# Making GpSimd work wait for the VectorE operation planned ahead of it (12 links in a one-core encoder layer)

## The chip, the cores and the metric

The kernel runs on one core of one Trainium2 chip. The metric is the device time of one execution in microseconds, from the first to the last work of the program; a trace of one profiled execution shows every instruction with its start and duration. Five engines work side by side, each through its own queue in order: TensorE (PE: matrix products and transposes), ScalarE (ACT), VectorE (DVE), GpSimd (POOL) and SyncE (SP, which issues nearly all DMA transfers here).

## The reference

One layer of a hybrid encoder, 512 tokens, width 1024, float32. An RMS norm and one wide input projection feed two branches; their gated sum goes through an output projection, and two normed residual additions close the layer.

```python
h = rms_norm(x, norm_pre[i])
(aq, ak, av, az, dq, dk, dv, db, da, dz, gate_att, gate_dn) = split_cols(h @ w_in[i])
...
o_att = gqa_attention(q, k, v)           # 8 heads, 2 kv heads, 128 wide
y_att = (o_att * jax.nn.silu(az)) @ w_br_att[i]
...
o_dn = bidir_gated_deltanet(qd, kd, vd, g, beta)   # 8 heads, chunks of 64, both directions
y_dn = (rms_norm(o_dn) * jax.nn.silu(dz)) @ w_br_dn[i]
mix = (jax.nn.sigmoid(gate_att) * y_att + jax.nn.sigmoid(gate_dn) * y_dn) @ w_out[i]
x = x + rms_norm(mix, norm_post[i])
x = x + rms_norm(jax.nn.sigmoid(x @ w_ple_gate[i]) * (p[i] @ w_ple_proj[i]), ple_norm[i])
```

In the delta rule each chunk needs a decay matrix exp(g_i - g_j) under a triangular mask, and the inverse of a unit triangular matrix.

## The kernel before

**Products in split form.** Every large product is made of three TensorE passes in fp32r: each operand is split into hi (rounded) and lo (the remainder). Activations lie transposed in SBUF as hi and lo; weights come as slabs of 128x1024 by DMA into `wraw`, two buffers. For each slab `split` (line 212) casts hi on ACT (`whi`) and subtracts lo = raw - hi (`wlo`), either on POOL (planned at 2.37 us) or on DVE (planned at 1.16 us), whichever is planned to end first, with a bias. `gemm_t` then issues 8 x 3 products of 512 columns per slab (lines 478 to 480). There are two `whi` and two `wlo` buffers, so that TensorE frees what the next split writes.

**The order of the work.** `Flow` is a planner written in Python. Generators for all parts of the layer (jobs of the weight stream in a fixed list, and side jobs for convolution tails, decay masks, the triangular inverse, attention heads and so on) call `op(engine, duration, ready time, function)`. The planner reserves the first free slot of that engine in planned time (`slot`, `fit`) and keeps the function in a heap; `flush` calls the functions in order of planned start (line 101, to which most trace rows are put down). So every engine's queue is in order of planned time; the real times differ. The framework adds semaphore waits only where data needs them.

**DVE and POOL.** `V` reserves DVE, `G` reserves POOL. `W` (line 171) reserves both for a DVE operation both of whose tensor inputs lie in SBUF: in planned time no POOL work stands beside it. The queues keep only the order on each engine, so in real time the two can still meet, or either can run ahead.

**The parts that the steps below touch.** `prep` (line 819) makes the decay masks, four tiles of 128x512 per head group g and direction d: a DMA brings a row broadcast (`u<-CI`), POOL masks it with `affine_select`, then either eight small exponentials on ACT (line 842) or one add on DVE (`exps2`, line 846, through `W`) and one exponential on ACT. `phase_a` (line 878) inverts the triangular blocks on DVE: 30 steps of a product and a subtraction (`step`, lines 928 and 930, through `W`), followed by transposes and TensorE block products (lines 972 to 1020). While this chain is planned, `split` prefers DVE. `conv_tail` runs four taps on DVE, a Tanh and one more DVE operation before TensorE transposes the result (line 713). `kv_tail` (line 1287) scales the rotated keys by their norms with a 128x256 product on DVE (through `W`), and TensorE transposes them (line 1309).

Of the kernel before, what the change touches and what calls it, by code (L numbers as in the profile page):

```python
# [11 lines left out]
AF = mybir.ActivationFunctionType  # L12
ALU = mybir.AluOpType
AX = mybir.AxisListType

S = 512
NT = 4
# [9 lines left out]
class Event:  # L27
    def __init__(self):
        self.t = None
# [5 lines left out]
class Flow:  # L35
# [7 lines left out]
    def __init__(self, slots):  # L43
        self.now = 0.0
        self.eng = {}
        self.slots = {k: [0.0] * n for k, n in slots.items()}
        self.parts = []
        self.later = []
        self.n = 0

    def spawn(self, gen, prio):
        ev = Event()
        self.n += 1
        self.parts.append([prio, self.n, gen, ("at", 0.0), ev])
        return ev
# [18 lines left out]

    def op(self, eng, dur, dep, fn, *a, **k):

        engs = eng if isinstance(eng, tuple) else (eng,)
        t, at = self.slot(engs, dur, dep)
        for e, i in zip(engs, at):
            self.eng[e].insert(i, (t, t + dur))  # L80
        if fn is not None:
            self.n += 1
            heapq.heappush(self.later, (t, self.n, fn, a, k))
        return t + dur

    def free(self, tag, t=None):
        self.slots[tag].append(self.now if t is None else t)
# [59 lines left out]
PR = dict(dec=5, dm1=7, y=9, conv=1, gate=0, kv=4, q=5, head=8, ple=5, prep=7, tab=9)  # L147
GAP = 0.0
EXPS = 0.0
X_DVE = ()  # L150
WARM = 8.2
W1 = 0
# [4 lines left out]
def layer(ctx, tc, x, p, wt, wba, wn, wpp, npre, rows, qkn, hd16, npost, pnorm, dnorm, cs, out):  # L157
    nc = tc.nc
    pe, act, dve, pool, sync = nc.tensor, nc.scalar, nc.vector, nc.gpsimd, nc.sync

    caps = {"wraw": 2, "whi": 2, "wlo": 2, "f2": 5, "c2": 4, "blk": 3, "gi": 2, "go": 2, "mm": 5, "aux": 3}
    F = Flow({**caps, **{f"u{i}": 1 for i in range(17)}})
    op, free, spawn = F.op, F.free, F.spawn

    def A(dur, dep, fn, *a, **k):
        return op("ACT", dur, dep, fn, *a, **k)

    def V(dur, dep, fn, *a, **k):
        return op("DVE", dur, dep, fn, *a, **k)

    def W(dur, dep, fn, *a, **k):

        return op(("DVE", "POOL"), dur, dep, fn, *a, **k)

    def G(dur, dep, fn, *a, **k):
        return op("POOL", dur, dep, fn, *a, **k)

    def Q(kb, dep, o, i, by=sync):

        t = op("DGE" if by is sync else "ACT", 0.46, dep, by.dma_start, o, i)  # L180
        return op("DMA", kb * 0.3, t + 0.5, None) + 1.3
# [6 lines left out]
    def tile(tag, shape, dt=F32):  # L188
        cnt[0] += 1
        return sb.tile(list(shape), dt, tag=tag, bufs=caps.get(tag, 1), name=f"{tag}_{cnt[0]}")  # L190

    def const(shape, name, dt=F32):
        return sb.tile(shape, dt, tag=name, bufs=1, name=name)

    def unit(i, shape, dt=F32):
        return tile(f"u{i}", shape, dt)
# [8 lines left out]
    def either(dep, *ways):  # L205

        w = min((F.fit(w[0], w[1], max(F.now + 0.2, dep + 0.15))[0] + w[1], i, w) for i, w in enumerate(ways))[2]
        return op(w[0], w[1], dep, *w[2:])
# [17 lines left out]
    def bc(a):  # L226
        return a.unsqueeze(2).to_broadcast([128, 4, 128])
# [333 lines left out]
    cj = const([128, 2, 4, 8, 2], "cj")  # L561
# [155 lines left out]
    def sumsq(pt, dst, dep=0.0):  # L717
        yield "get", "f2"
        sq = tile("f2", [128, 4, 128])
        ta = A(0.5, dep, act.activation, sq, pt, AF.Square)  # L720
        t = V(0.62, ta, dve.reduce_sum, dst, sq, axis=AX.X)
        free("f2", t)
# [88 lines left out]
    def r32(i):  # L811
        return slice(32 * i, 32 * i + 32)
# [6 lines left out]
    def prep(g, d):  # L819


        away = (g, d) == (1, 1)
        yield "ev", dec_ev
        if g == 1:
            yield "ev", E_ev[0, 1]
            yield "ev", sub_ev if d else spilled
        u = 16 if away else LTu[g, d]
        yield "get", f"u{u}"
        lt = unit(u, [128, 16, 128])
        sgn = 1 if d == 0 else -1  # L830
        for c in range(NT):
            E = lt[:, 4 * c:4 * c + 4, :]
            t = Q(2, late["CI"], E, CI[d, c, 4 * g:4 * g + 4].unsqueeze(0).to_broadcast([128, 4, 128]))
            yield "at", t - 1.0
            t = G(0.66, t, pool.affine_select, out=E, in_=E, compare_op=ALU.is_ge, fill=-1e30, base=0,
                  pattern=[[0, 4], [sgn, 128]], channel_multiplier=-sgn)

            def exps(E=E, c=c):
                for h in range(4):
                    for i in range(2):  # L840
                        e = E[:, h, i * 64:i * 64 + 64]
                        act.activation(e, e, AF.Exp, bias=cj[:, d, c, 4 * g + h, i:i + 1])

            def exps2(E=E, c=c):
                Eh = E.rearrange("p h (s i) -> p h s i", s=2)
                dve.tensor_add(Eh, Eh, cj[:, d, c, 4 * g:4 * g + 4, :].unsqueeze(3).to_broadcast([128, 4, 2, 64]))

            ta = F.fit("ACT", 1.94, max(F.now + 0.2, t + 0.15))[0] + 1.94
            tv = F.slot(("DVE", "POOL"), 0.68, t)[0] + 0.68
            if ta <= F.fit("ACT", 0.57, tv + 0.15)[0] + 0.57 + EXPS:  # L850
                t = A(1.94, t, exps)
            else:
                t = A(0.57, W(0.68, t, exps2), act.activation, E, E, AF.Exp)
            if away:
                t = Q(2, t, E1[c], E)
            tE[g, d, c] = t
        if away:
            free("u16", t)
            spilled.set(F.now)
            yield "get", f"u{LTu[g, d]}"  # L860
            lt = unit(LTu[g, d], [128, 16, 128])
            for c in range(NT):
                tE[g, d, c] = Q(2, tE[g, d, c], lt[:, 4 * c:4 * c + 4, :], E1[c])
        LTs[g, d] = lt
        yield "ev", nj_ev[g]
        for c in range(NT):
            E = lt[:, 4 * c:4 * c + 4, :]

            def scaled(E=E, c=c):
                for h in range(4):  # L870
                    act.activation(E[:, h, :], E[:, h, :], AF.Copy, scale=Nj[:, g, d, c, h:h + 1])

            tE[g, d, c] = either(tE[g, d, c], ("POOL", 1.05, pool.tensor_mul, E, E, bc(Nj[:, g, d, c])), ("ACT", 1.25, scaled))
        E_ev[g, d].set(F.now)
# [3 lines left out]
    def phase_a(g):  # L878
# [11 lines left out]
        for c in range(NT):  # L890
# [11 lines left out]
            for d in range(2):  # L902
                E = LT[d][:, 4 * c:4 * c + 4, :]
                t = V(0.62, tE[g, d, c], dve.tensor_mul, AT[g][d][:, 4 * c:4 * c + 4, :], qk, E)
                t = V(0.62, t, dve.tensor_mul, E, kk, E)
# [10 lines left out]
        t = Q(4, t2, dB[64:128].rearrange("(s q) j i -> q j s i", q=4).rearrange("q j s i -> (q j) s i"), lb)  # L916
# [3 lines left out]
        b, w, tt = (tile("blk", [128, 32, 32]) for _ in range(3))  # L920
        t = Q(4, max(tl + [t]), b, dB)
        yield "at", t - 0.5
        t = W(0.65, t, dve.tensor_scalar, out=w, in0=b, scalar1=-1.0, scalar2=None, op0=ALU.mult)
        t = W(0.15, t, dve.memset, w.rearrange("p a b -> p (a b)")[:, 0:1024:33], 1.0)

        def step(m):
            sh = [128, m, 31 - m]
            dve.tensor_tensor(out=tt[:, 0:m, 0:31 - m], in0=b[:, 0:m, m:m + 1].to_broadcast(sh),
                              in1=w[:, m:m + 1, m + 1:].to_broadcast(sh), op=ALU.mult)
            dve.tensor_sub(w[:, 0:m, m + 1:], w[:, 0:m, m + 1:], tt[:, 0:m, 0:31 - m])  # L930

        chains[0] += 1
        if g == 0:
# [1 line left out]
        for m in range(30, 0, -1):  # L935
            t = W(0.32 + 2 * m * (31 - m) * 0.00104, t - 0.1, step, m)
            yield "at", t - 1.0
        chains[0] -= 1
        t = Q(4, t, dW, w)
# [38 lines left out]
        t = A(0.5, 0.0, act.copy, M, m1)  # L978
# [11 lines left out]
        for d, P, Q_ in combos:  # L990
            t = V(0.62, 0.0, dve.tensor_scalar, out=LT[d][r32(P), :, r32(Q_)], in0=v1[r32(P)], scalar1=-1.0,
                  scalar2=None, op0=ALU.mult)
# [6 lines left out]
        for i in range(2):  # L999
# [9 lines left out]
            t = A(0.5, 0.0, act.copy, M2[:, 8 * i:8 * i + 8, :], m2)  # L1009
# [4 lines left out]
        for i in range(2):  # L1014
            yield "get", "aux"
            v3 = bank("aux", [128, 8, 64])
            for s in range(8):
# [3 lines left out]
                if s % 4 == 3:  # L1021
                    yield "pe", 0.62
                    yield "at", F.now + GAP
            t = V(0.62, 0.0, dve.tensor_scalar, out=LT[0][r64[0], 8 * i:8 * i + 8, r64[1]], in0=v3[r64[0]], scalar1=-1.0,
                  scalar2=None, op0=ALU.mult)
# [261 lines left out]
    def kv_tail(t, o, tev):  # L1287
# [7 lines left out]
        tq = A(0.35, 0.0, act.activation, sq, ks, AF.Square)  # L1295
        ts = V(0.35, tq, dve.reduce_sum, sak[:, t, :], sq, axis=AX.X)
        free("f2", ts)
# [88 lines left out]
    def att_head(h):  # L1386
# [14 lines left out]
        for t in range(NT):  # L1401
# [8 lines left out]
            rs = saq[:, t, h:h + 1]  # L1410
            te = V(0.62, 0.0, dve.reduce_max, mx, sc, axis=AX.X)
            te = V(0.15, te, dve.tensor_scalar, out=bi, in0=mx, scalar1=rs, scalar2=-1.0, op0=ALU.mult, op1=ALU.mult)
# [370 lines left out]
    for j in jobs:  # L1783
        f, a = j[0], tuple(j[1:])
# [77 lines left out]
```

## Time and profile before

| | |
|---|---|
| timed runs | median 771.64 us of 3 (769.33 to 776.71) |
| the profiled execution | 770.75 us, its span 769.0 us |
| busy PE, DVE, ACT, POOL | 753.4, 470.6, 344.4, 306.6 us |
| granted TensorE clock | 0.995 of full speed |

How to read the rows: start and duration in us; then engine, line, operation, tiles written and read (buffer numbers left out), shape and count. A bracket gives the engine's idle time ahead of the instruction and what ended it. Most lines are 101, where the planner calls each function; so the tile names tell the rows apart. Recorded spans on POOL are rough, and ends of products are modelled.

### The profile page before, as it was taken

The page shows a single profiled execution, that of the slowest core. Times are in us where ns is not written, and L with a number is a line of the kernel's source. Part 1 is how long each engine was busy: PE and PEld are TensorE (multiplying, and loading weights), DVE is VectorE, ACT ScalarE, POOL GpSimd, SP SyncE. Part 2 cuts the span into 40 slices and gives each one's busy share as a digit, 9 for nine tenths or more (in the row PEclk, how much of TensorE's full clock was granted, in tenths as well). Part 3 has the DMA queues.
Part 4 walks back from the last instruction along what each step waited for, and adds up shares of the span by engine and source line. Part 5 has one row for each costly group of instructions (what it writes and reads, how often), then busy time and mean ns, then how long its engine had stood idle before and what let it go on. Part 6 is the DMA issues. An engine that isn't in the chain of part 4 may idle for free.

```text
span 769.0 us, 11946 instructions
## 1 busy us (share of the span) xinstructions
PE 753.4 (98%) x4566; PEld 632.5 (82%) x4566; DVE 470.6 (61%) x910; ACT 344.4 (45%) x636; POOL 306.6 (40%) x276
## 2 busy tenths in 40 slices
PE   9998999999999999999999999999999999999995
PEld 7877888888879888888779988787888888888885
DVE  4548779978574667889494643637666753413434
ACT  6566563644544235332443145335566632332422
POOL 5255395311433227200441145556555424661511
PEclk9999999999999999999999999999999999999999
DMA  7453225664521224635521133424443256552313
GB/s 280 141 181 110 82 76 161 213 202 167 151 96 42 74 91 125 198 117 164 151 72 42 42 110 125 131 101 154 149 141 120 97 152 217 200 165 115 96 65 113
DMA packets 53899, 100.51 MB, mean 131 GB/s; under 512 B 21009, under 2 KB 21969, under 8 KB 53842
## 3 DMA queue, kind: packets, MB, share of 16 engines
q1 hardware_dynamic: 53554, 99.49, 39.7%
q8 instruction: 36, 0.59, 0.3%
q10 hardware_dynamic: 288, 0.26, 0.1%
q14 instruction: 21, 0.17, 0.1%
HBM read 80.83 MB, written 18.91 MB: 130 GB/s over the span
## 4 chain that ended last, share of the span: by engine, by line
PE 90%; DVE 4%; issue 2%; ACT 1%; POOL 1%; DMA 1%; POOLq 0%; DVEq 0%; SPq 0%; ACTq 0%
PE mm L478 15%; PE mm L480 15%; PE mm L479 15%; PE mm L498 4%; PE mm L500 4%; PE mm L499 4%; PE mm L516 3%; PE mm L517 3%; PE mm L518 2%; PE aux L1074 2%; PE mm L1434 2%; PE aux L1106 2%; PE aux L1054 1%; DVE f L101 1%; PE aux L1092 1%
## 5 line engine op out<-in xcount | busy, mean ns | idle before, releaser
L101 POOL TENSOR_TENSOR wlo<-wraw,whi 128x1024 fp32r<-128x1024 f32 x67 | 160.4, 2394 | 300.5 <-ACT whi L101 296.5
L478 PE MATMUL mm<-u,wlo 128*128 128x512 f32 x568 | 229.9, 405 | 2.0 <-POOL wlo L101 2.0
L480 PE MATMUL mm<-u,whi 128*128 128x512 f32 x568 | 222.1, 391 | 0.0
L479 PE MATMUL mm<-u,whi 128*128 128x512 f32 x568 | 221.4, 390 | 0.0
L101 ACT CAST whi<-wraw 128x1024 fp32r<-128x1024 f32 x84 | 88.2, 1050 | 130.8 <-PE mm L480 89.3
L480 PEld LDWEIGHTS mm<-u,whi 128*128 128x128 f32 x568 | 106.6, 188 | 23.3
L478 PEld LDWEIGHTS mm<-u,wlo 128*128 128x128 f32 x568 | 106.9, 188 | 22.1 <-POOL wlo L101 2.8
L479 PEld LDWEIGHTS mm<-u,whi 128*128 128x128 f32 x568 | 107.0, 188 | 19.3
L101 DVE SCALAR_TENSOR_TENSOR f<-mm,cw,f 128x510 f32<-128x510 f32 (+1 forms) x96 | 71.9, 749 | 22.5 <-ACT f L101 19.9
L101 DVE TENSOR_TENSOR u<-aux,u 128x512 fp32r<-128x512 f32 (+2 forms) x68 | 44.5, 672 | 27.9 <-ACT u L101 20.4
L498 PE MATMUL mm<-u,u 128*128 128x512 f32 (+1 forms) x136 | 52.0, 383 | 0.0
L500 PE MATMUL mm<-u,u 128*128 128x512 f32 (+1 forms) x136 | 51.4, 378 | 0.0
L499 PE MATMUL mm<-u,u 128*128 128x512 f32 (+1 forms) x136 | 51.2, 377 | 0.0
L101 POOL TENSOR_TENSOR u<-wraw,u 128x1024 fp32r<-128x1024 f32 x16 | 38.3, 2398 | 13.4 <-ACT u L101 13.3
L516 PE MATMUL mm<-whi,u 128*128 128x512 f32 x96 | 38.2, 398 | 0.0
L518 PE MATMUL mm<-whi,u 128*128 128x512 f32 x96 | 37.5, 391 | 0.0
L517 PE MATMUL mm<-wlo,u 128*128 128x512 f32 x96 | 37.5, 390 | 0.0
L101 ACT COPY c<-aux 128x512 f32<-128x512 f32 x18 | 10.6, 587 | 58.7 <-DVE f L101 36.4
L101 ACT CAST u<-aux 128x512 fp32r<-128x512 f32 (+1 forms) x36 | 20.0, 564 | 35.1 <-PE aux L1607 14.0
L101 ACT ACTIVATE f<-mm 128x512 f32<-128x512 f32 (+1 forms) x38 | 20.9, 562 | 24.5 <-PE mm L713 9.8
L101 ACT ACTIVATE mm<-f 128x512 f32<-128x512 f32 x24 | 14.4, 601 | 38.0 <-DVE f L101 34.1
L500 PEld LDWEIGHTS mm<-u,u 128*128 128x128 f32 x136 | 25.6, 188 | 4.9
(254 smaller groups left out, 1298.3 us busy)
## 6 DMA issues: line engine op xcount, KB each, us to landing
wraw<-in_wt_dram SPq DMA_DIRECT2D x72, 512.0 KB, 3.4
wraw<-in_wn_dram SPq DMA_DIRECT2D x28, 512.0 KB, 3.9
u<-CI SPq DMA_DIRECT2D x16, 256.0 KB, 4.7
u<-in_x_dram SPq DMA_DIRECT2D x4, 512.0 KB, 7.4
eD<-c SPq DMA_DIRECT2D x8, 256.0 KB, 2.3
gate_dz<-go SPq DMA_DIRECT2D x8, 256.0 KB, 2.0
gate_gB<-go SPq DMA_DIRECT2D x8, 256.0 KB, 2.3
gate_gA<-go SPq DMA_DIRECT2D x8, 256.0 KB, 2.0
```

The lines of the kernel that those rows point to most:

```text
L101: fn(*a, **k)
L478: pe.matmul(o, lo[:, k, :], mh(k), start=(k == 0), stop=False)
L479: pe.matmul(o, hi[:, k, :], ml(k), start=False, stop=False)
L480: pe.matmul(o, hi[:, k, :], mh(k), start=False, stop=(k == 7))
L498: pe.matmul(o, b, hi, start=(i == 0), stop=False)
L499: pe.matmul(o, a, lo, start=False, stop=False)
L500: pe.matmul(o, a, hi, start=False, stop=(i == 7))
L516: pe.matmul(o[t], b, hi, start=(k == 0), stop=False)
L517: pe.matmul(o[t], a, lo, start=False, stop=False)
L518: pe.matmul(o[t], a, hi, start=False, stop=(k == 7))
L1074: pe.matmul(pw[:, h, :], Vm[g][d][:, 4 * c + h, :], r[:, h, :], start=True, stop=True)
L1106: pe.matmul(oa[:, h, :], AT[g][d][:, 4 * c + h, :], w[:, h, :], start=True, stop=True)
```

## The change: a wait from POOL on the DVE operation planned close ahead

Where a POOL operation of at least 0.6 us (planned) is issued, and the last issued DVE operation that reserved both engines was planned to end less than 1.5 us ahead of its planned start, the POOL instruction gets an explicit semaphore dependency on that DVE instruction. The order on every engine and all planned times stay. `exps2` and `step` now return their last instruction, so that it can be waited for. The rule passes over POOL functions that return no instruction (the small norm helpers).

```diff
+SYNC = mybir.DependencyInfo(mybir.DependencyClass.Sync, mybir.DependencyReason.DATA)
...
+        self.shut, self.link = None, lambda a, b: None
...
         if fn is not None:
             self.n += 1
+            if eng == "POOL" and dur >= LONG:
+                fn = self.behind(t, fn)
+            elif engs[1:] == ("POOL",):
+                fn = self.shutting(t + dur, fn)
             heapq.heappush(self.later, (t, self.n, fn, a, k))
         return t + dur
+
+    def shutting(self, end, fn):
+        def f(*a, **k):
+            self.shut = end, fn(*a, **k)
+        return f
+
+    def behind(self, t, fn):
+        def f(*a, **k):
+            ins = fn(*a, **k)
+            if ins is not None and self.shut and self.shut[1] is not None and t - self.shut[0] < NEAR:
+                self.link(ins, self.shut[1])
+        return f
...
+LONG, NEAR = 0.6, 1.5
...
+    def link(later, ahead):
+        tc.add_manual_dep(later.ins, ahead.ins.name, SYNC, reason="not beside each other")
+
+    F.link = link
...
-                dve.tensor_add(Eh, Eh, cj[:, d, c, 4 * g:4 * g + 4, :].unsqueeze(3).to_broadcast([128, 4, 2, 64]))
+                return dve.tensor_add(Eh, Eh, cj[:, d, c, 4 * g:4 * g + 4, :].unsqueeze(3).to_broadcast([128, 4, 2, 64]))
...
-            dve.tensor_sub(w[:, 0:m, m + 1:], w[:, 0:m, m + 1:], tt[:, 0:m, 0:31 - m])
+            return dve.tensor_sub(w[:, 0:m, m + 1:], w[:, 0:m, m + 1:], tt[:, 0:m, 0:31 - m])
```

The change is described as touching 36 places. Walked through on the planner's list, the rule selects 12 in one program: eight `affine_select` of `prep` and four `wlo` subtractions.

## Rows read from the trace of the kernel before

**Rows 1.** The page, busy time of each engine: busy us, share, instructions
```profile
PE 753.4 (98%) x4566; PEld 632.5 (82%) x4566; DVE 470.6 (61%) x910; ACT 344.4 (45%) x636; POOL 306.6 (40%) x276
```

**Rows 2.** Timeline of TensorE, the stalls that DVE or POOL ended
```profile
56.99 0.50 PE L478 MATMUL mm<-u,wlo 128*128 128x512 f32 x1 [0.67 <-POOL wlo L101]
...
66.68 0.66 PE L713 MATMUL mm<-ident,u 128*128 128x128 f32 x4 [0.76 <-DVE u L101]
...
71.41 0.50 PE L478 MATMUL mm<-u,wlo 128*128 128x512 f32 x1 [1.31 <-POOL wlo L101]
...
400.44 0.44 PE L1309 MATMUL aux<-ident,f 128*128 128x128 f32 x2 [1.40 <-DVE u L101]
...
495.55 0.63 PE L1168 MATMUL mm<-ident,u 128*128 128x128 f32 x4 [0.82 <-DVE u L101]
```

**Rows 3.** Timeline of POOL, 51 to 62 us
```profile
51.62 0.63 POOL L101 TENSOR_SCALAR_AFFINE_SELECT u<-u 128x512 f32<-128x512 f32 x1
...
54.54 2.40 POOL L101 TENSOR_TENSOR wlo<-wraw,whi 128x1024 fp32r<-128x1024 f32 x1 [2.28 <-issue]
...
59.24 2.40 POOL L101 TENSOR_TENSOR wlo<-wraw,whi 128x1024 fp32r<-128x1024 f32 x1
```

**Rows 4.** Timeline of DVE, 51 to 66 us
```profile
51.64 1.16 DVE L846 TENSOR_TENSOR u<-u,cj 128x512 f32<-128x512 f32 x1 [0.42 <-POOL u L101]
...
59.46 2.74 DVE L846 TENSOR_TENSOR u<-u,cj 128x512 f32<-128x512 f32 x1
...
65.12 0.68 DVE L846 TENSOR_TENSOR u<-u,cj 128x512 f32<-128x512 f32 x1
```

**Rows 5.** Timeline of POOL, 394 to 405 us
```profile
397.39 2.38 POOL L101 TENSOR_TENSOR wlo<-wraw,whi 128x1024 fp32r<-128x1024 f32 x1
```

**Rows 6.** Timeline of DVE, 394 to 405 us
```profile
395.27 0.42 DVE L101 TENSOR_TENSOR f<-f,sak 128x256 f32<-128x256 f32 x1
...
397.99 2.06 DVE L101 TENSOR_TENSOR f<-f,sak 128x256 f32<-128x256 f32 x1
```

**Rows 7.** Timeline of POOL, 143 to 180 us
```profile
165.06 0.64 POOL L101 TENSOR_SCALAR_AFFINE_SELECT u<-u 128x512 f32<-128x512 f32 x1 [11.72 <-DVE blk L928]
...
175.37 1.58 POOL L101 TENSOR_SCALAR_AFFINE_SELECT u<-u 128x512 f32<-128x512 f32 x1 [1.53 <-DMA u<-CI]
```

**Rows 8.** Timeline of DVE, 143 to 180 us
```profile
166.79 0.39 DVE L930 TENSOR_TENSOR blk<-blk,blk 128x220 f32<-128x220 f32 x1
167.09 0.68 DVE L846 TENSOR_TENSOR u<-u,cj 128x512 f32<-128x512 f32 x1
...
173.87 0.69 DVE L846 TENSOR_TENSOR u<-u,cj 128x512 f32<-128x512 f32 x1 [2.25 <-POOL u L101]
...
175.24 1.22 DVE L101 TENSOR_TENSOR wlo<-wraw,whi 128x1024 fp32r<-128x1024 f32 x1
```

**Rows 9.** Timeline of ACT, 48 to 70 us
```profile
52.83 0.63 ACT L101 ACTIVATE u<-u 128x512 f32<-128x512 f32 x1 [0.40 <-DVE u L846]
53.37 1.03 ACT L101 CAST whi<-wraw 128x1024 fp32r<-128x1024 f32 x1
...
62.23 0.63 ACT L101 ACTIVATE u<-u 128x512 f32<-128x512 f32 x1 [1.47 <-DVE u L846]
...
65.30 0.60 ACT L101 ACTIVATE mm<-f 128x512 f32<-128x512 f32 x1 [0.52 <-DVE f L101]
...
67.80 1.03 ACT L101 CAST whi<-wraw 128x1024 fp32r<-128x1024 f32 x1
```

**Rows 10.** Timeline of TensorE, the first product with three of the slabs
```profile
63.04 0.39 PE L478 MATMUL mm<-u,wlo 128*128 128x512 f32 x1
...
177.55 0.39 PE L478 MATMUL mm<-u,wlo 128*128 128x512 f32 x1
...
407.42 0.48 PE L478 MATMUL mm<-u,wlo 128*128 128x512 f32 x1
```

**Rows 11.** One stretch: us, busy of PE, PEld, DVE, ACT, POOL, clock, DMA
```profile
143.00:193.00 50.00, 50.00 (x226) 41.36 (x225) 43.25 (x90) 24.99 (x52) 7.25 (x7) 1.00 0.61 199
```

## The prediction

> **What bounds the kernel now.** I read the page's busy times first: TensorE has work for 753.4 of 769.0 us [rows 1]. The other engines are at 40 to 61%, so an edit on VectorE (DVE) or GpSimd (POOL) pays only where TensorE stands still for them. The second view is TensorE's own timeline, searched for stalls that a DVE or POOL instruction ended. There are five [rows 2]: 0.67 us at 56.99 and 1.31 us at 71.41 for a POOL weight remainder (wlo), 0.76 at 66.68, 1.40 at 400.44 and 0.82 at 495.55 for a DVE operation. Their sum, 4.96 us, is about all that any change in the order of DVE and POOL can give; no other stall over 0.15 us was ended by either of them. The third view is the timelines of POOL, DVE and ScalarE (ACT) around the places touched.
>
> **Which places.** The planner is a fixed calculation, so the rule of the change can be walked through on the plan of before. It selects 12 POOL operations in one program (36 is three times that): eight `affine_select`, four weight subtractions. In the profiled run they fall into four kinds.
> (a) POOL started first and the DVE operation met it: 51.62 beside 51.64, 59.24 beside 59.46, 397.39 beside 397.99 [rows 3, 4, 5, 6].
> (b) DVE started first and POOL sat behind it anyway: three of the `affine_select` at 151 to 176, which took 1.3 to 1.6 us in place of 0.64 (1.58 at 175.37, behind the DVE subtraction of 175.24) [rows 7, 8].
> (c) The POOL operation was over before the planned DVE operation began, since DVE ran late: three places, 147.25, 149.05 and 165.06; the last stands in [rows 7], its DVE operation ran 166.79 to 167.18 [rows 8].
> (d) The DVE operation was long done: three places, 54.54 among them [rows 3].
>
> **Part 1, what (a) returns.** The masked decay add on DVE takes 0.68 us undisturbed, at 65.12, and took 1.16 at 51.64 and 2.74 at 59.46 [rows 4]: 0.48 and 2.06 lost to POOL. The 256-column product takes 0.42 at 395.27 and took 2.06 at 397.99 [rows 6]: 1.64 lost.
> *At 51.6:* the add ends 0.48 earlier. ACT waits for it at 52.83, casts whi at 53.37 right behind, and POOL's subtraction at 54.54 follows the cast's end (54.40) by 0.14 [rows 3, 9]. The delayed `affine_select` moves DVE's second add by 0.3, to an end near 53.7, still ahead of 54.1. So that wlo comes about 0.4 earlier, and of the stall of 0.67 about 0.4 goes.
> *At 59.2:* DVE's add ends near 60.14 in place of 62.20; the conv taps behind it start 2 us earlier. ACT, which sat 1.47 us at 62.23 for this add, goes on at 60.8; its Tanh at 65.30 comes to 63.4 [rows 9]. The transposes at 66.68 wait for the DVE operation behind that Tanh, so their 0.76 goes altogether. The next cast, at 67.80, comes up to 2 us earlier, and with it the wlo for which TensorE stalls at 71.41; TensorE itself arrives 0.4 + 0.76 earlier, so of the 1.31 about 0.85 goes. Price: POOL's own subtraction starts at about 60.2 and ends at 62.6 in place of 61.64; its slab is first used at 63.04 [rows 10], by 24 products counted from 56.99. The 0.4 left just covers it; if cover fails, TensorE stalls by what is missing, under 1 us. Behind it on POOL stands one `affine_select`, whose reader runs only at 66.55. POOL issues no DMA here; the weight load that SyncE starts when this subtraction ends moves by 1 us and is cast near 70, so it is hidden. Sum to 72 us: 0.4 + 0.76 + 0.85 = 2.0.
> *At 397.4:* the product ends near 398.4 and TensorE, done with its row of products at 399.04, doesn't stall at 400.44 [rows 2]: 1.4 gained. POOL's subtraction ends at 400.85 in place of 399.77; its slab is used at 407.42 [rows 10], so 6.6 us hide it. Behind it wait POOL's small scale operations, about 0.1 late.
>
> **Part 2, what the waits cost.** No row shows such a wait's own price. The nearest is the 0.14 from an ACT end to the POOL start it releases [rows 3, 9]; the lower bound is nothing, since in kinds (b) and (d) POOL starts no earlier today. Twelve times 0.14, 1.7 us, is the upper bound, were all on the path; none is, by the slacks above, so I take nothing. In (c) POOL now starts 2.1 us later each time, and DVE's next add, which needs that mask and is in order, waits with all behind it: at 167.09 [rows 8] it would come at about 167.7 (the chain step that met the mask at 165.20 gets 0.35 back first). Of the two others the same count gives -0.2 and +0.7. TensorE doesn't stall anywhere between 72 and 215 us; slabs made by DVE are ready 0.45 to 2.9 us ahead, 1.09 for the one subtracted at 175.24 and used at 177.55 [rows 8, 10]. Half a microsecond of DVE lateness is thus hidden there, and DVE's idle 2.25 at 173.87 [rows 8] absorbs some. In the stretch 143 to 193 DVE is busy for 43.25 of 50 us [rows 11], however, with a 30-step chain whose result TensorE takes in at 211 us, with no slack that I can see. A TensorE that arrives 2.0 earlier there can find DVE not 2.0 earlier. So the first gain lies between 0 and 2.0; I take 1.3, nearer the top because the ACT casts that DVE waits for move with TensorE.
>
> **A rule weighed.** The rows show the second to start waiting for the first: the add at 59.46 ended 0.55 after POOL's 61.64. [...]
>
> **Sum.** 1.3 + 1.4 = 2.7 us. The profiled execution took 770.75 us (span 769.0), so 768.0. The median of the three timed runs, 771.64, lies 0.9 above it, and the same subtraction from it gives 768.9; I stay with 768.0.
>
> **The rivals.**
> *More is gained.* All of the 2.0 is kept and the stall at 495.55 goes too: 770.75 - 4.2 = 766.5. For it: the casts follow TensorE. Against: nothing touched lies near 495. Chance 0.12.
> *No difference: the gain is given back.* TensorE runs ahead of its weights, the early gain dies at 211 and the later one at a slab that comes late after 400; nothing is kept of the 2.7, 770.75 - 0 = 770.8. For it: DVE's load in 143 to 193. Against: weights are cast when TensorE frees their buffer, so they follow it. Also here: the waits don't do what they say, because engine starts shift by some tenths between executions and (a) need not recur. Chance 0.24.
> *Slower: DVE waits for POOL that waits for DVE.* In the three places of (c) the new wait strings mask, add and chain together. Were the whole POOL delay, 2.17 + 2.04 + 2.12 = 6.3 us, passed on, less 1.09 of slack at 175.24, TensorE would lose 5.2, and with only the gain at 400 left: 770.75 + 5.2 - 1.4 = 774.6. It decides once DVE is over 1.09 us late at 175.24. For it: DVE is nearly full there. Against: the add waits only 0.6 to 0.9 by the count above, and 2.25 idle comes before 175.24. Chance 0.10.
> The forecast, a gain of 1.5 to 3.5 us, has the remaining 0.54.
>
> **How the numbers follow.** The forecast and the first two rivals hold 0.90 and their times lie between 766.5 and 770.8; runs of one kernel differ by more (769.33 to 776.71 before), so I set 764.5 to 773.5, which leaves out the slower case and far runs. Measurement can tell about 1%, 7.7 us, from no change. Faster than that needs more than all stalls in sight: 0.03. Slower than that needs the slower case at more than its price, every late POOL operation of (a) to (c), 16 us together, mostly unhidden: 0.03. Within 1%: 0.94.
>
> **What would show it.** Right: the adds at 51.6 and 59.5 and the product at 398 take 0.68, 0.68 and 0.42, each with its POOL operation behind; TensorE's stalls at 66.7 and 400 are gone and that at 71.4 is halved; the chain's DVE stretch shows idle of 0.6 to 0.9 before two adds, ended by POOL. Wrong: a new TensorE stall at 63 (subtraction late), at 150 to 180 (DVE late), or at 211 (the chain late), or any slab in that stretch that DVE delivers after TensorE asks.

## The result and the profile after

The median fell from 773.46 us (10 runs, 769.33 to 776.71) to 768.19 (10 runs, 765.57 to 771.05): a ratio of 0.9934, interval 0.9912 to 0.9957, so 3.3 to 6.8 us. A second measurement of the same kernel (below) gave 0.9967, interval 0.9949 to 0.9985. Both intervals hold the stretch from 0.9949 to 0.9957, 3.3 to 3.9 us; that is a rough common value and no interval of its own. The forecast was 2.7 us and 768.0. The change lies within the 1% that the prediction called no change, though both intervals leave out a ratio of 1.

The page after, the busy times [rows 1]. The profiled execution took 769.0 us:

```profile
span 767.3 us, 11952 instructions
...
PE 753.6 (98%) x4566; PEld 633.0 (82%) x4566; DVE 466.2 (61%) x910; ACT 344.1 (45%) x636; POOL 303.6 (40%) x276
```

DVE lost 4.4 us of busy time and POOL 3.0 without losing an instruction: the time in which one sat behind the other. TensorE's busy time is unchanged (753.4 and 753.6 us for the same 4566 products); what can have shrunk is its idle time.

The DVE operations that met POOL before [rows 4, 6, 8], timeline of DVE after:

```profile
51.09 0.69 DVE L873 TENSOR_TENSOR u<-u,cj 128x512 f32<-128x512 f32 x1 [0.95 <-POOL u L102]
...
58.45 0.68 DVE L873 TENSOR_TENSOR u<-u,cj 128x512 f32<-128x512 f32 x1
...
148.95 0.69 DVE L873 TENSOR_TENSOR u<-u,cj 128x512 f32<-128x512 f32 x1 [0.74 <-POOL u L102]
...
164.60 0.69 DVE L873 TENSOR_TENSOR u<-u,cj 128x512 f32<-128x512 f32 x1 [0.87 <-DMA wraw<-in_wt_dram]
...
397.39 0.43 DVE L97 TENSOR_TENSOR f<-f,sak 128x256 f32<-128x256 f32 x1
```

And their partners, timeline of POOL after [rows 3, 5, 7]:

```profile
51.85 0.63 POOL L102 TENSOR_SCALAR_AFFINE_SELECT u<-u 128x512 f32<-128x512 f32 x1 [0.79 <-DVE u L873]
...
59.27 2.41 POOL L102 TENSOR_TENSOR wlo<-wraw,whi 128x1024 fp32r<-128x1024 f32 x1 [1.05 <-issue]
...
163.93 0.63 POOL L102 TENSOR_SCALAR_AFFINE_SELECT u<-u 128x512 f32<-128x512 f32 x1 [12.45 <-DVE blk L957]
...
397.95 2.40 POOL L102 TENSOR_TENSOR wlo<-wraw,whi 128x1024 fp32r<-128x1024 f32 x1 [1.13 <-issue]
```

Read the two in pairs. The adds took 1.16 and 2.74 us before and the product 2.06; now 0.69, 0.68 and 0.43, and POOL starts 0.07, 0.14 and 0.13 us behind their ends (51.78, 59.13, 397.82). Note that for the subtractions at 59.27 and 397.95 the bracket says "issue", though the wait added here is what held them: that a start follows a DVE end by 0.14 is seen only by laying the two engines side by side.

TensorE's timeline after, its stalls [rows 2] and the products around 210 us:

```profile
55.92 0.50 PE L505 MATMUL mm<-u,wlo 128*128 128x512 f32 x1 [0.68 <-POOL wlo L102]
...
68.35 0.50 PE L505 MATMUL mm<-u,wlo 128*128 128x512 f32 x1 [0.28 <-POOL wlo L102]
...
207.67 1.29 PE L999 MATMUL aux<-blk,u 32*32 32x32 f32 x128
...
210.47 1.02 PE L1012 MATMUL aux<-u,c 32*32 32x32 f32 x96
...
213.10 0.45 PE L1012 MATMUL aux<-u,c 32*32 32x32 f32 x32 [1.62 <-issue]
...
398.05 0.39 PE L507 MATMUL mm<-u,whi 128*128 128x512 f32 x1
398.28 0.38 PE L1336 MATMUL aux<-ident,f 128*128 128x128 f32 x2
...
493.54 0.63 PE L1195 MATMUL mm<-ident,u 128*128 128x128 f32 x4 [1.01 <-DVE u L122]
```

Of the five stalls of before, the 0.76 at 66.68 and the 1.40 at 400.44 are gone, the 1.31 at 71.41 is 0.28, and those at 57 and 495 stay. A stall that [rows 2] did not list, because neither DVE nor POOL ended it, has grown to 1.62 us at 213.10. Following the n-th product of one trace to the n-th of the other gives the balance. TensorE is 1.02 us earlier at 14 us, ahead of any link; 3.06 earlier at 71; 2.17 earlier at 213; 0.60 at 218; 2.16 at 400; 1.96 at the end. So the early links gave 2.04 us, 2.46 were lost between 210 and 218, and the link at 398 gave 1.56.

### The profile page after: what moved, and what is told of

Read it like the earlier page. It is cut to its first block, busy times and chain, and to the rows that moved or that the text cites. A ratio compares the mean times of both kernels' runs of the same rounds, so it can differ in the third digit from the quotient of the medians.

```text
span 767.3 us, 11952 instructions
## 1 busy us (share of the span) xinstructions
PE 753.6 (98%) x4566; PEld 633.0 (82%) x4566; DVE 466.2 (61%) x910; ACT 344.1 (45%) x636; POOL 303.6 (40%) x276
## 4 chain that ended last, share of the span: by engine, by line
PE 89%; DVE 1%; ACT 1%; issue 1%; DMA 1%; POOL 0%; POOLq 0%; DVEq 0%; SPq 0%; ACTq 0%
PE mm L505 16%; PE mm L507 16%; PE mm L506 16%; PE mm L527 4%; PE mm L525 4%; PE mm L526 4%; PE mm L543 3%; PE mm L544 3%; PE mm L545 3%; PE aux L1101 2%; PE mm L1461 2%; PE aux L1133 2%; PE aux L1081 1%; PE aux L1119 1%; PE aux L1092 1%; PE mm L740 1%
```

## The experiments

All experiments but the last three leave the plan, the instructions and their order alone and only choose which of the 12 links are made: `link` is called for the m-th selected place if m is in a list. Places 1 to 3 lie at 51 to 59 us, 4 to 10 (the masks beside the triangular inverse) at 146 to 174, 11 and 12 at 366 and 397.

```diff
+                self.m += 1
+                if self.m in KEEP:
-                self.link(ins, self.shut[1])
+                    self.link(ins, self.shut[1])
```

**early**, the first three links alone.

```diff
+KEEP = (1, 2, 3)
```

> Only the three links before 62 us. Theory A (the gain is the TensorE stalls that GpSimd and VectorE cause near 57, 67, 71 and 400 us, and the mask links near 150 to 175 are free): the adds at 51.6 and 59.5 take 0.68 us, TensorE is 2.0 us earlier by 72 us than it was relative to its start of products, the stall at 400 stays at 1.4; total 1 to 2 us faster than before, ratio 0.997 to 0.999. Theory B (the mask links matter, because they keep GpSimd from the steps of the chain): under 1 us. Theory C (no part alone shows; before varies between executions): ratio 1.000.

Measured: 769.23 us against 772.35, ratio 0.9962, interval 0.9946 to 0.9979: 1.6 to 4.2 us, where 1 to 2 was expected. TensorE's timeline in this run:

```profile
56.06 0.50 PE L508 MATMUL mm<-u,wlo 128*128 128x512 f32 x1 [0.34 <-POOL wlo L102]
...
68.48 0.50 PE L508 MATMUL mm<-u,wlo 128*128 128x512 f32 x1 [0.24 <-POOL wlo L102]
...
212.61 0.45 PE L1015 MATMUL aux<-u,c 32*32 32x32 f32 x32 [0.97 <-issue]
...
398.30 0.44 PE L1339 MATMUL aux<-ident,f 128*128 128x128 f32 x2 [1.39 <-DVE u L124]
```

The stalls of 57 and 71 shrink and that of 66.7 is gone, while the one at 400 stays at 1.39: each link acts at its own place. At 212.61 only 0.97 us are lost, not 1.62.

**late**, the link at 397 alone.

```diff
+KEEP = (12,)
```

> Only the link near 397 us. Theory A: the key product at 398 takes 0.42 us and the stall of 1.4 us at 400 goes; nothing else changes, the stalls of 0.76 and 1.3 us near 67 and 71 stay; 1.4 us faster, ratio 0.998. Theory B: the same 1.4 us, since it says nothing of this place. Theory C: 1.000.

Measured: 769.36 against 772.35, ratio 0.9959, interval 0.9941 to 0.9977: 1.8 to 4.6 us where 1.4 was expected. TensorE's timeline:

```profile
65.98 0.66 PE L743 MATMUL mm<-ident,u 128*128 128x128 f32 x4 [0.74 <-DVE u L124]
...
70.70 0.50 PE L508 MATMUL mm<-u,wlo 128*128 128x512 f32 x1 [1.28 <-POOL wlo L102]
```

The early stalls are back as they were [rows 2], and nothing stalls at 400. Followed product by product, this trace gives back 1.6 us there, and loses about 1 us at the stall of 495, which the link doesn't touch. What the timed runs give beyond 1.6 has no place in this trace.

**masks**, places 4 to 10 alone, where the prediction saw only a price.

```diff
+KEEP = (4, 5, 6, 7, 8, 9, 10)
```

> Only the seven links on affine_select between 145 and 176 us. Theory A: the masks start 0.07 us behind their VectorE operation, the chain ends within 0.5 us of where it ended, TensorE doesn't stall in the stretch; 0 +/- 0.5 us, ratio 1.000. Theory B: the chain ends about 1 us earlier and 1 to 3 us come off the total, ratio 0.996 to 0.999. Rival slower: VectorE waits for masks and TensorE for slabs at 150 to 180; 1 to 5 us slower, ratio 1.001 to 1.007.

Measured: 770.88 against 772.35, ratio 0.9982, interval 0.9966 to 0.9998. The rival that strings DVE and POOL together is out: nothing is slower. In the trace the 30-step chain ends 0.3 us later than before, and all of TensorE's stalls stay, the one at 400 among them:

```profile
400.68 0.44 PE L1339 MATMUL aux<-ident,f 128*128 128x128 f32 x2 [1.41 <-DVE u L124]
```

So a gain of 0.2 to 2.6 us is measured, where Theory A expected 0 within 0.5 and Theory B 1 to 3. The size fits B, its mechanism doesn't, since the chain ends no earlier; no row shows how the gain could arise. That stays open.

**early_late**, all but places 4 to 10.

```diff
+KEEP = (1, 2, 3, 11, 12)
```

> All links but the seven on affine_select between 145 and 176 us. Theory A: as fast as the whole change, 2.7 to 5 us faster than before, ratio 0.993 to 0.997. Theory B: 1 to 3 us slower than the whole change.

Measured: 768.22 against 772.35, ratio 0.9932, interval 0.9911 to 0.9952. Without the seven mask links the gain is that of the whole change as first measured (0.9934), so what masks showed is not needed for it. Of the five, 2 and 11 are of kind (d) and no run took them alone. With six timed runs the interval is wide.

**none**, the control: the changed program with no link made, so the instructions and waits of before.

```diff
+KEEP = ()
```

> A control: the code of the change with no link kept, so that every engine's instructions and waits are those of before. Theory A: ratio 1.000 within its interval (the excess of about 1 us that each part alone showed over its stall is scatter). Rival (an offset between a new kernel and before in the way they are timed): 0.998 to 0.9985, and 1 to 1.4 us must be taken off every part's gain. The adds and the product take 1.16, 2.74 and 2.06 us again.

Measured: 771.68 against 771.58, ratio 0.9994, interval 0.9974 to 1.0014. No offset shows, but the interval also holds the 0.998 to 0.9985 of the rival, so it doesn't rule one out by itself. Set directly beside the control, which shares any such offset, the 12 times of after_again (below) lie 2.9 us lower on the mean (768.66 against 771.55), 1.7 to 4.1 by a 95% interval. That much comes from the waits and from nothing else in the change. TensorE's timeline:

```profile
63.66 0.66 PE L743 MATMUL mm<-ident,u 128*128 128x128 f32 x4 [0.71 <-DVE u L124]
...
68.38 0.50 PE L508 MATMUL mm<-u,wlo 128*128 128x512 f32 x1 [1.28 <-POOL wlo L102]
...
212.70 0.45 PE L1015 MATMUL aux<-u,c 32*32 32x32 f32 x32 [1.16 <-issue]
...
398.42 0.44 PE L1339 MATMUL aux<-ident,f 128*128 128x128 f32 x2 [1.41 <-DVE u L124]
```

It also answers a doubt of the prediction, whether engine starts shift between executions so that the meetings of kind (a) need not recur. They do recur: 1.17 and 2.74 us for the two adds and 2.05 for the product in this second execution of the old order, from DVE's timeline of this run:

```profile
56.43 2.74 DVE L876 TENSOR_TENSOR u<-u,cj 128x512 f32<-128x512 f32 x1
...
395.98 2.05 DVE L97 TENSOR_TENSOR f<-f,sak 128x256 f32<-128x256 f32 x1
```

**after_again**, the changed kernel itself once more, beside the control and on the same chip.

> The change once more, for its second trace. Theory A: ratio 0.992 to 0.996 again; no collision over 0.5 us on VectorE; the stall inside the second block product at about 213 us is again 0.7 to 1.6 us, ended about 1.4 us after the instruction fetch of 16 KB has landed; the drop of TensorE's clock behind it may or may not come back.

Measured: 768.13 against 771.58, ratio 0.9967, interval 0.9949 to 0.9985: 1.2 to 3.9 us. Its stall at 213 measured 1.90 us.

**early_again** and **late_again**, the same two parts once more.

> Only the three links before 62 us, once more. Theory A: 2.0 us at 72 us, less what the stall at 213 us takes back, 0.3 to 0.9 us and sometimes a drop of the clock: 0.5 to 2 us faster, ratio 0.9975 to 0.9995. Rival (more than the stalls is gained): 0.996 again.

> Only the link near 397 us, once more, since the first measurement gave 3.2 us (1.8 to 4.6) for a stall of 1.4 us. Theory A with scatter: 1 to 2.5 us faster, ratio 0.997 to 0.9985. Rival (the wait gives back more than the stall that a trace shows): 0.996 again.

Measured: early_again 769.37 against 771.62, ratio 0.9970 (0.9952 to 0.9988), late_again 770.11 against 771.62, ratio 0.9969 (0.9954 to 0.9985). Together with the first runs, early is worth between 1.6 and 3.7 us (both intervals hold 0.9952 to 0.9979) and late between 1.8 and 3.6 (0.9954 to 0.9977). The forecast had 1.3 and 1.4. In the repeat the stall at 213 was 0.78 with the early links.

**spread**: can the loss at 213 be had back? The 128 small products there are issued in four parts, with a planned gap behind each.

```diff
-GAP = 0.0
+GAP = 0.3
```

> The change, and the small block products of each inverse issued in quarters with one step of a large product between them. If the stall of 1.62 us at 213 us (and 0.35 at 383) is TensorE waiting for its own instructions, it shrinks to under 0.3 us, because the small products no longer use them up at 10 ns each: 1 to 3 us faster than the change, ratio to before 0.990 to 0.993. If it is a wait for data, it stays, and the inverse ends later: same or 1 us slower than the change.

Measured: 796.83 against 771.58, ratio 1.0327, interval 1.0297 to 1.0356. The stalls at 213 and 383 are gone, but the gaps move what the planner places later. Busy time by stretch (columns: us, busy of PE, PEld, DVE, ACT and POOL with their instructions, granted clock, DMA share, GB/s), spread first, then the changed kernel:

```profile
430.00:480.00 50.00, 38.00 (x261) 34.24 (x261) 24.43 (x75) 9.50 (x17) 2.53 (x2) 0.93 0.08 27
```

```profile
430.00:480.00 50.00, 50.00 (x273) 42.78 (x272) 23.23 (x56) 20.39 (x40) 20.93 (x17) 1.00 0.34 108
```

TensorE idles for 12 us of 50 where it never did before, among operations of the recurrence that other work used to fill; DMA carries 27 GB/s there in place of 108. A local cure that goes through the planner changes the whole order.

**v1_gap**: the same cure with one gap, in the middle of the second block product of each inverse only, on top of the change.

```diff
-                yield "at", F.now + GAP
+                yield "at", F.now + (0.3 if s == 7 else GAP)
```

> The change, and in the second block product of each inverse one step of a large product put in at half, ahead of the quarter in which TensorE stalled for 0.7 to 1.9 us. Theory (TensorE waits for its own instructions there): the stall at 213 us is under 0.8 us and no drop of the clock follows; up to 2 us faster than the change, ratio to before 0.990 to 0.995, unless the order behind it, which the planner lays anew from there, costs as much as it did with all quarters spread. Rival (a wait for data): the stall stays at 1.6.

Measured: 767.08 against 771.62, ratio 0.9940, interval 0.9915 to 0.9965; the profiled span is 764.0 us. It is the fastest median here, but its interval overlaps that of the change, so it is not shown to be faster. TensorE's timeline, and the stretch around it:

```profile
210.44 0.75 PE L1012 MATMUL aux<-u,c 32*32 32x32 f32 x64
...
212.02 0.90 PE L1012 MATMUL aux<-u,c 32*32 32x32 f32 x64
```

```profile
210.00:220.00 10.00, 10.00 (x167) 7.87 (x166) 8.39 (x12) 3.82 (x6) 4.62 (x2) 1.00 0.23 81
```

With large products issued between the halves TensorE doesn't stall, and the clock stays at 1.00 through the stretch.

**gate_first**: the stall at 495 is named for a DVE operation, but that one stood behind a gate load. The first gate load of each head group is asked for ahead of a planned wait.

```diff
+        ahead = yield from gate_in("dz", 4 * g)
...
-            zt, tz = yield from gate_in("dz", 4 * g + h)
+            zt, tz = ahead if h == 0 else (yield from gate_in("dz", 4 * g + h))
```

> The change, and the first gate tile of each half of the delta branch loaded before the wait for the scaled output in place of after it. The stall of 0.6 to 1.9 us at 494 us, whose VectorE operation waited up to 4.1 us for that load, goes: 0.6 to 1.5 us faster than the change, ratio to before 0.991 to 0.9935.

Measured: 770.20 against 771.58, ratio 0.9985, interval 0.9965 to 1.0006. A miss: with all links in place, it is slower on the mean than after_again, which was measured with it, by 1.7 us (0.5 to 3.0). DVE's timeline in this run:

```profile
494.06 0.76 DVE L122 SCALAR_TENSOR_TENSOR mm<-mm,dnn,gi 128x512 f32<-128x512 f32 x1 [4.51 <-DMA gi<-gate_dz]
```

DVE waits 4.51 us for the gate, and TensorE's stall behind it is 2.13. Before it waited 3.20, but in the control, without this step, 4.50: the wait varies by itself. Nor did the step bring the load forward in real time. SyncE issues it here, and in the control, by its timelines:

```profile
488.42 0.42 SPq L122 DMA_DIRECT2D gi<-gate_dz  x1
```

```profile
487.00 0.38 SPq L124 DMA_DIRECT2D gi<-gate_dz  x1
```

That is 1.1 us before DVE falls idle (489.55 and 488.10) in both. So the experiment didn't test an earlier load. What the traces show of the stall at 495 is that it ends with this load, and that DVE starts 4.3 us behind the issue before and 5.6 in the control and here. Why the load takes longer in one execution than in another is open. The planner also laid out anew what follows from 300 us on.

## Why the prediction was right, and where its steps were not

**What bounds the kernel, and the places.** Held. In the traces only stalls of TensorE, and its clock, moved the time; the 12 places were those found by walking through the plan, and the time came from places of kind (a) alone.

**Part 1, at 51.6.** Of the 0.67 about 0.4 was to go; in the trace after, 0.68 stays. The step that failed is "the add ends 0.48 earlier, ACT waits for it". The add did end earlier, but in this execution ACT stood behind its own exponentials, by its timeline after [rows 9]:

```profile
49.85 2.03 ACT L869 ACTIVATE u<-u,cj 128x64 f32<-128x64 f32 x8 [0.43 <-POOL u L102]
...
52.36 1.03 ACT L122 CAST whi<-wraw 128x1024 fp32r<-128x1024 f32 x1
```

They had waited 0.43 for a mask, and so the cast kept its place. In seven other traces with this link the stall is 0.34, 0.36, 0.43, 0.19, 0.77, 0.68 and 0.30; in five without it 0.67, 0.52, 0.86, 0.72 and 0.85. On the mean it falls from 0.72 to 0.47 over all thirteen; in one execution the gain is not certain.

**Part 1, at 59.2.** Held, by its own steps: the add takes 0.68, the Tanh and the transposes behind it come earlier, the 0.76 goes, and 1.31 becomes 0.28 where 0.45 was forecast. The sum to 72 us was to be 2.0 and is 2.04, but its parts are 0.04, 0.98 and 1.02 us in place of 0.4, 0.76 and 0.85, so that it agrees so well is partly luck. POOL's delayed subtraction did not uncover a slab: no stall at 63.

**Part 1, at 397.** Held: 1.4 forecast, the stall is gone, 1.56 in the shift of products, and 1.6 in all five traces with this link and an unchanged plan. The forecast took stalls at the number in the bracket, which is a little too small: it counts from the recorded end of the product before, 0.39 us behind its start, while without a stall the next one starts after 0.23 (398.05 and 398.28 above). So a stall that goes gives back some 0.16 more than its bracket: 1.40 and 0.16 are the 1.56.

**Part 2, the price of the waits.** Held. The waits of DVE on masks in the inverse were put at -0.2, +0.7 and +0.6; those adds now wait 0.14, 0.74 and 0.87 (the profile puts the last down to a DMA, but the mask it reads ended at 164.56, 0.04 ahead of it). TensorE doesn't stall between 72 and 207, as the slacks said. They do cost DVE a little. The same 89 operations of DVE, up to the end of the chain, in the trace before and in the trace after (columns as above):

```profile
143.77:193.00 49.23, 49.23 (x223) 40.72 (x222) 42.52 (x89) 24.67 (x51) 7.25 (x7) 1.00 0.61 200
```

```profile
140.66:190.24 49.58, 49.58 (x224) 41.02 (x223) 42.33 (x89) 24.76 (x51) 4.44 (x7) 1.00 0.61 199
```

DVE is busy in them for 0.19 us less and takes 0.35 longer from the first to the last. In early_late, without the mask links, it takes 49.23 again. POOL's seven operations get 2.8 us shorter.

**The step that failed:** "a 30-step chain whose result TensorE takes in at 211 us, with no slack that I can see", by which DVE would not follow TensorE and 0.7 of the first 2.0 would be lost. DVE did follow, but for 0.34 us. Its last step of the chain, by its timeline before and after:

```profile
192.81 0.19 DVE L930 TENSOR_TENSOR blk<-blk,blk 128x30 f32<-128x30 f32 x1
```

```profile
190.05 0.19 DVE L957 TENSOR_TENSOR blk<-blk,blk 128x30 f32<-128x30 f32 x1
```

The chain ended at 193.00 and at 190.24, 2.76 earlier, where TensorE was 3.10 earlier; the first block product that needs it starts more than 17 us later, without a stall, in both traces, at 210.76 and at 207.67. So there was slack that the prediction didn't see. TensorE's timeline before:

```profile
210.76 1.29 PE L972 MATMUL aux<-blk,u 32*32 32x32 f32 x128
...
213.56 1.02 PE L985 MATMUL aux<-u,c 32*32 32x32 f32 x96
...
215.27 0.45 PE L985 MATMUL aux<-u,c 32*32 32x32 f32 x32 [0.69 <-issue]
```

The place was right and the mechanism was not. What was lost there was lost inside the second block product, three quarters of the way through a run of 128 small products, by a wait that no other engine ended ("issue"). It was there before the change with 0.69 us; it is 1.62 after, 0.93 more. The rest is the clock. Stretches of the trace after, then of the one before (columns as above):

```profile
210.00:213.10 3.10, 1.49 (x99) 1.02 (x97) 1.88 (x3) 1.12 (x2) 2.35 (x1) 1.00 0.25 88
213.10:218.00 4.90, 4.90 (x45) 3.92 (x46) 4.61 (x8) 0.60 (x1) 0.00 (x0) 0.65 0.37 110
```

```profile
215.30:220.00 4.70, 4.70 (x51) 3.91 (x52) 4.42 (x7) 0.60 (x1) 0.76 (x1) 1.00 0.37 115
```

Behind the longer stall the granted clock averages 0.65 over 4.9 us; it is 0.50 from 214 to 217, where the products of 512 columns start 0.43 us apart in place of 0.23, and 1.57 us go there. Behind the shorter one it stays at 1.00. In this one pair of traces the early gain was lost altogether by 218 us.

It is not lost in every execution. The stall at 213 measures 0.78, 0.79, 0.97, 1.61, 1.62 and 1.90 us with the early links, and 0.64, 0.69, 0.69, 0.98 and 1.16 without them: 1.28 against 0.83 on the mean, in ranges that overlap. (The 0.79 is from gate_first, whose plan is that of the change up to 300 us; v1_gap and spread differ there and are left out.) The clock fell behind two of the first six (0.83 over 210 to 220 us in both); it is 1.00 there in the three others with the unchanged plan and in all five without the links. Followed product by product from 50 us on, the six are 2.1 us further ahead at 72 on the mean and have lost 1.1 of it by 220, most of it in the two with a fall (2.5 and 2.8, against 0.1 to 0.9); the other five shift by less than 0.2 on the mean at either place. Against these, about 1.2 us stays.

So the term "I take 1.3" came out near what the traces show, for a reason that did not apply. The sum in the traces is 1.2 + 1.6 = 2.8 us. The timed runs of early keep 1.6 at least, and both measurements of the whole allow 3.3 to 3.9; after_again against the control gives 1.7 to 4.1. Whether more is gained than the traces show is open: six traces don't tell how often the clock falls in the timed runs.

**The rivals.** The gain given back (770.8) is out by both intervals, and for its second half, that the meetings need not recur, by the control. The string of waits (774.6) is out by masks. More gained (766.5) needed the stall at 495 to go; it is 1.01 in the trace after, 0.82 before and 2.12 in the control, which has the same waits, so it varies by itself.

**The forecast of 768.0** came near the measured 768.19 with some luck: the sum was subtracted from one profiled execution of 770.75 us, and the median of before later came out at 771.6 to 773.5 in larger samples.

## What to carry to other kernels

Where two engines are given work side by side of which the later lasts until the earlier has ended (here a DVE add of 0.68 us took 2.74), and one of the two is on the path, tie the uncritical one behind it with an explicit wait: here, where the wait was what held POOL, it started 0.07 to 0.20 us behind the DVE operation, while a meeting cost the critical engine up to 2.06 us, and 5 of 12 links gave all of the gain that can be told apart. Price such a change by the stalls of the bounding engine that end with the operations concerned, compare busy times over the same operations rather than over the same microseconds, and look too at the stalls that no engine ends, since the time gained must pass them. Don't judge a change of a few microseconds by the difference of two profiled spans: here the executions differed by 2.9 us before the first changed instruction ran.

## What the runs showed of the hardware

**Stalls in a run of small products.** The stall at 213 ends with nothing that another engine did. The trace after shows an instruction transfer of 0.02 MB in that time, in the transfers of 210.2 to 211.8 us (columns: packets, MB, share of 16 engines):

```profile
q8 instruction: 1, 0.02, 5.5%
```

5.5% of 16 engines over 1.6 us is 1.4 us of one engine; in the packed trace the packet has 16384 bytes and takes 1.42 us. A run of 128 small products takes 1.29 us at 207.67, about as long as such a transfer. The times of these packets, which the packed traces hold, put the stall beside them: TensorE goes on 1.36 us behind the end of the packet in the trace before (213.91 and 215.27) and 1.40 in the trace after (211.71 and 213.10), though the stall was 0.69 in one and 1.62 in the other. That the stall is TensorE waiting for its instructions is the author's reading. It fits these times and v1_gap, where large products between the halves make the stall vanish, but no row names it as the cause, so it is argued and not shown.

**The clock behind single stalls.** At 213 it fell behind stalls of 1.62 and 1.90 us (after and after_again, 0.83 over 210 to 220), and not behind 1.61 (early_late, 1.00 over 210 to 220). At 495 it fell behind 2.12, in the control (columns as above):

```profile
490.00:500.00 10.00, 7.88 (x30) 6.11 (x29) 2.90 (x4) 2.12 (x3) 2.39 (x1) 0.83 0.40 127
```

and not behind 1.74, in late:

```profile
485.00:500.00 15.00, 13.26 (x65) 10.69 (x64) 5.59 (x10) 4.97 (x7) 5.68 (x4) 1.00 0.52 169
```

nor behind 2.13, in gate_first, where TensorE goes on at 496.31:

```profile
496.00:506.00 10.00, 9.69 (x45) 8.11 (x46) 1.62 (x3) 2.03 (x3) 4.79 (x2) 1.00 0.18 59
```

So stalls of nearly one length cost some 1.6 us more in one execution and nothing more in another, and what decides it no run here shows.

**The start of an execution.** The first 15 us of the changed kernel and of the control, which run the same instructions there:

```profile
0.00:15.00 15.00, 13.48 (x55) 10.71 (x56) 5.50 (x9) 9.37 (x16) 7.04 (x31) 0.89 0.78 301
```

```profile
0.00:15.00 15.00, 13.48 (x65) 10.73 (x66) 6.30 (x10) 9.08 (x16) 6.78 (x31) 1.00 0.83 310
```

TensorE's clock was 0.89 in one and 1.00 in the other, and the control did 65 products in place of 55. Of the 11 traces other than those of spread and gate_first, early_late alone is like the control; the other nine show 0.89. Set against the trace of before (0.89 too) the control is 2.93 us ahead at 14 us, and ends with a span of 770.2 against 769.0 all the same. Part of the scatter of the timed runs may be of this kind; that was not tried.

**The exclusion itself.** In the control the add that met POOL takes 2.74 us, from 56.43 to 59.17, and in the trace after, at 58.45, where POOL is idle from 58.22 to 59.27, 0.68. It shows the other way round too: before, the `affine_select` of 175.37 took 1.58 us, to 0.49 behind the end of the DVE subtraction of 175.24, and in the trace after all seven beside the inverse take 0.63 or 0.64. That the later operation stands still until the earlier ends is read from such times; no row says it.
